# Mem loaded first, biases loaded as rows, two w_mem slices in buffers of their own

## The chip, the cores and the metric

The kernel runs on one core of one Trainium2 chip. The metric is the device time of one execution in microseconds (us). Three runs of the kernel before took 675.11, 677.58 and 680.07 us, so the median is 677.58 us. A difference of about 1% (6.8 us) is what such runs can tell from no change.

## The reference, cut to what matters

The program computes one layer of a hybrid encoder on x (1024 x 1024, float32) and a memory mem (256 x 1024).

```
h    = layer_norm(x, ln_in_g, ln_in_b)
proj = h @ w_in + b_in                 # D_IN = 3912 columns, split among four head groups
       A: gated mixing   B: band attention   C: indexer, top 256 keys, attention   M: attention into mem
km, vm = split(mem @ w_mem_kv, 2)      # w_mem_kv is 1024 x 512
mixed  = concat(ya*silu(a_g), yb*silu(bg), yc*silu(cg), ym*silu(mg))
out    = layer_norm(2**0.25 * h + mixed @ w_out + b_out, ln_g, ln_b)
```

Only the first lines matter here: the norm of x, the product of mem with w_mem_kv, and the first columns of the projection (the indexer's key and head weights, `I_K`, and the first half of the gate of group M, `M_G`). ln_in_b and b_in are added per column of h and of proj. As h and proj are held turned round (columns on the 128 partitions), each bias is a number per partition.

## The kernel before, in words

Every large product is made with three matmuls per 128 rows of contraction: each float32 operand is split into a rounded part and a rest, and high x high, high x low and low x high are accumulated. `wblock` (L194) loads one slice of 128 weight columns (512 KB) into `raw`, a tag with two buffers, and splits it in two halves of 128x512 into `wblk`: ScalarE (ACT) copies the rounded part, GpSimd (POOL) subtracts it (L208). A third slice can be loaded only when POOL has finished with the first.

The work at the start is this. The loop over `FIRST_LOADS` (L359) issues the first transfers on SyncE's queue (SP): row blocks of x (`xt`, 128 rows, 512 KB each), the vector ln_in_g spread over all partitions (`g_in`), two halves of mem (`mt`) and the first two slices of w_mem, in the order x g m x m w x w x. Then come `b_col` (ln_in_b, L368) and `load_biases` (L146): four transfers whose source is read with neighbouring numbers going to neighbouring partitions, so that every number is a piece of 4 bytes; VectorE (DVE) makes `hbias`, half of `bias`, in three instructions.

`mem_parts` turns mem with TensorE (PE) and splits it into mT (ACT copies, DVE subtracts). `x_rows` (L290) norms one row block: two statistics instructions, an aggregate, a scaled subtraction (all DVE), the reciprocal root on POOL (`rs`, two instructions), and a scaling on ACT. `kv_of_mem` multiplies mem with the slices of w_mem; each call with i = 0 loads slices 2 and 3 from inside its loop. `x_parts` (L304) turns four normed row blocks, eight times four transposes into a PSUM bank, and from each bank ACT writes `hTh` and DVE writes `hTl`, with b_col as bias. A half of 512 positions needs all four of its row blocks before the first of its eight columns can be written. `ik_half` and `gate_half` are the first projections; they are called for half 0, then `x_rows` of blocks 4 to 7, the second `x_parts`, and the same projections for half 1.

Loads of x blocks 4 to 7 are kept behind the load of w_mem slice 3 (`issue_after(loads[3])`, L406); their `x_rows` are kept behind the last `hTl` of half 0 (`issue_after(first_half[0])`, L409). The order on each engine is otherwise written by a planner that runs before compilation: it walks the program with its own estimates of durations and takes the instruction with the best priority that is ready, where earlier program text has the better priority and a boost can be given (`high_priority`). Each engine then works through its list in that order and waits where an input is late.

Of the kernel before, what the change touches and what calls it, by code (L numbers as in the profile page):

```python
# [11 lines left out]
F32 = mybir.dt.float32  # L12
# [7 lines left out]
ALU = mybir.AluOpType  # L20
# [4 lines left out]
P = 128  # L25
NB = 8
KT = 8
# [18 lines left out]
OB, LB = 400, 0  # L46
LG_AT = 0
PRELOAD = (6,)
FIRST_LOADS = "xgmxmwxwx"
ML_V = (6,)  # L50
HR_V = 6
LB_V = (7, 6)
# [21 lines left out]
def f32(ap):  # L74
    return ap.bitcast(F32)
# [3 lines left out]
def tile_trunk(ctx, tc, x, mem, ln_in_g, ln_in_b, w_in, b_in, a_ln_g, a_ln_b, a_ws, a_bs,  # L79
               b_rel_rev, t5_table, w_mem, w_out, b_out, ln_g, ln_b, bucket1h, out):  # L80
    nc = tc.nc
    G, SP = nc.gpsimd, nc.sync
# [20 lines left out]
    PE, V, S = Engine(nc.tensor), Engine(nc.vector), Engine(nc.scalar)  # L103

    def run(steps):

        while True:
            try:
                next(steps)
            except StopIteration as e:  # L110
                return e.value

    cp = ctx.enter_context(tc.tile_pool(name="cp", bufs=1))
    gp = ctx.enter_context(tc.tile_pool(name="gp", bufs=1))
# [4 lines left out]
    ident = cp.tile([P, P], F32, name="ident")  # L119
# [8 lines left out]
    def bcast(t, vec):  # L128
        n = vec.shape[-1]
        SP.dma_start(out=t, in_=bass.AP(tensor=vec.tensor, offset=vec.offset, ap=[[0, P], [1, n]]))  # L130
# [5 lines left out]


    col = {}
    bias = cp.tile([P, 31], F32, name="bias")
    hbias = cp.tile([P, 31], F32, name="hbias")  # L140
    spans = ((0, 26, P), (I_K, 1, 72), (M_Q, 4, P))
    for c0, n, _ in spans:
# [1 line left out]
            col[c0 + t * P] = len(col)  # L144

    def load_biases():  # L146
        V.memset(hbias, 0.0)
        for c0, n, m in spans:
            a = col[c0]
            SP.dma_start(out=bias[:m, a:a + n], in_=b_in[c0:c0 + n * m].rearrange("(t p) -> p t", p=m))  # L150
            V.tensor_scalar(hbias[:m, a:a + n], bias[:m, a:a + n], 0.5, None, ALU.mult)

    h_dram = [dp.tile([P, DM], F32, name=f"h_dram{r}") for r in range(NB)]

# [15 lines left out]
    def s4(name, dt=F32R, shape=(P, SEQ)):  # L170
        return gp.tile(list(shape), dt, tag="s4", bufs=S4, name=name)
# [11 lines left out]
    E = ep.enter_context(tc.tile_pool(name="ep", bufs=1))  # L183

    def ev(name, bufs=EV):
        return E.tile([P, 512], F32, tag="ev", bufs=bufs, name=name)

    def bank(tag, name=None):
        return ps.tile([P, 512], F32, tag=tag, bufs=BANKS[tag], name=name or tag)


    loads = []

    def wblock(w, c0, m=P):  # L194

        raw = E.tile([P, KT, P], F32, tag="raw", bufs=2, name="raw")
        loads.append(SP.dma_start(out=raw[:, :, :m], in_=w[:, c0:c0 + m].rearrange("(k p) c -> p k c", p=P)).ins)
        ts = []
        if m < P:
            narrow = [gp.tile([P, 2, KT // 2, m], F32R, tag=tag, bufs=1, name="wnar") for tag in ("planes", "score6")]  # L200
        for q in range(2):
            t = E.tile([P, 2, 4, P], F32R, tag="w", bufs=WB, name="wblk") if m == P else narrow[q]
            r = raw[:, 4 * q:4 * q + 4, :m]
            if WH[0] <= len(loads) < WH[1]:
                G.tensor_scalar(t[:, 0], r, 1.0, 0.0, ALU.mult, ALU.add)
            else:
                S.activation(t[:, 0], r, AF.Copy)
            G.tensor_sub(t[:, 1], r, f32(t[:, 0]))  # L208
            ts.append(t)
        return ts  # L210

    def project(t, a, b, m=P, hi=hh, lo=hl, tag="pp"):

        acc = bank(tag, "acc")
        for k in range(KT):
            wh, wl = t[k // 4][:, 0, k % 4, :m], t[k // 4][:, 1, k % 4, :m]
            PE.matmul(acc[:m, :b - a], wh, hi(k, a, b), start=(k == 0), stop=False)
            PE.matmul(acc[:m, :b - a], wh, lo(k, a, b), start=False, stop=False)
            PE.matmul(acc[:m, :b - a], wl, hi(k, a, b), start=False, stop=(k == KT - 1))
            yield  # L220
        return acc
# [56 lines left out]


    g_in = s4("g_in", F32)  # L280
    b_col = cp.tile([P, KT], F32, name="b_col")
    mT = [s4(f"mT{i}", F32R, (P, 4, 256)) for i in range(4)]

    def x_load(rb):
        tag = ("S", "S", "S", "S", "s4", "score7", "v3", "v3")[rb]
        xt = gp.tile([P, DM], F32, tag=tag, bufs={"S": SB, "v3": 2, "s4": S4}.get(tag, 1), name="xt")
        SP.dma_start(out=xt, in_=x[rb * P:(rb + 1) * P, :])
        return xt

    def x_rows(rb, xt):  # L290

        st = E.tile([P, 2, 6], F32, tag="st", bufs=2, name="st")
        V.bn_stats(st[:, 0], xt[:, :512])
        V.bn_stats(st[:, 1], xt[:, 512:])
        mv = E.tile([P, 2], F32, tag="mv", bufs=2, name="mv")
        V.bn_aggr(mv, st)
        rs = E.tile([P, 1], F32, tag="rs", bufs=2, name="rs")
        with tc.high_priority(offset=BOOST):
            rstd_of(mv[:, 1:2], rs)
        V.scalar_tensor_tensor(xt, xt, mv[:, 0:1], g_in, ALU.subtract, ALU.mult)  # L300
        with tc.high_priority(offset=BOOST):
            S.activation(xt, xt, AF.Copy, scale=rs)

    def x_parts(half, xts):  # L304

        high, rest = hT[half]
        for k in range(KT):
            pt = bank(("pt", "qk")[k % 2], "xT")
            for j in range(4):
                PE.transpose(pt[:, j * P:(j + 1) * P], xts[j][:, k * P:(k + 1) * P], ident)  # L310
            begin = S.activation(high[:, k, :], pt, AF.Identity, bias=b_col[:, k:k + 1])
            end = V.scalar_tensor_tensor(rest[:, k, :], pt, b_col[:, k:k + 1], f32(high[:, k, :]), ALU.add, ALU.subtract)
        return end.ins, begin.ins
# [6 lines left out]
    def mem_parts(r, mt):  # L320
        for q in range(2):
            pt = bank("pt")
            for j in range(4):
                k = 4 * q + j
                PE.transpose(pt[:, j * P:(j + 1) * P], mt[:, k * P:(k + 1) * P], ident)
            src, dst = pt.rearrange("p (a b) -> p a b", a=4), slice(r * P, (r + 1) * P)
            S.activation(mT[q][:, :, dst], src, AF.Copy)
            V.tensor_sub(mT[2 + q][:, :, dst], src, f32(mT[q][:, :, dst]))
# [29 lines left out]
    xts, mts, w_kv = [], [], []  # L358
    for what in FIRST_LOADS:  # L359
        if what == "x":  # L360
            xts.append(x_load(len(xts)))
        if what == "m":
            mts.append(mem_load(len(mts)))
        if what == "w":
            w_kv.append(wblock(w_mem, len(w_kv) * P))
        if what == "g":
            bcast(g_in, ln_in_g)
    SP.dma_start(out=b_col, in_=ln_in_b.rearrange("(t p) -> p t", p=P))  # L368
    load_biases()
    for r in range(2):  # L370
        mem_parts(r, mts[r])
    for rb in range(4):
        x_rows(rb, xts[rb])
    def kv_of_mem(i):

        t = ev("kv")
        for pair in range(2):
            acc = run(project(w_kv[2 * i + pair], 0, 256, P, mhi, mlo))
            S.activation(t[:, pair * 256:pair * 256 + 256], acc[:, :256], AF.Copy)
            if not i:  # L380
                w_kv.append(wblock(w_mem, 256 + pair * P))
        return t

    km = kv_of_mem(0)
    first_half = x_parts(0, xts)
    vm = kv_of_mem(1)


    wik = wblock(w_in, I_K, 72)
    wmg = wblock(w_in, M_G)  # L390
    ikh = s4("ikh")
# [3 lines left out]
    def ik_half(a, b):  # L395
        acc = run(project(wik, a, b, 72))
        bk = col[I_K]
        with tc.high_priority(offset=BOOST):
            for lo in (0, 64):
                S.activation(ikh[lo:lo + 64, a:b], acc[0:64, :], AF.Identity, bias=bias[0:64, bk:bk + 1])  # L400
            S.activation(iwT[64:72, a:b], acc[64:72, :], AF.Identity, bias=bias[64:72, bk:bk + 1])
            for lo in (0, 64):
                V.scalar_tensor_tensor(ikl[lo:lo + 64, a:b], acc[0:64, :], bias[0:64, bk:bk + 1],
                                       f32(ikh[0:64, a:b]), ALU.add, ALU.subtract)

    with tc.issue_after(loads[3]):  # L406
        xts += [x_load(rb) for rb in range(4, NB)]
    ik_half(0, 512)
    with tc.issue_after(first_half[0]):  # L409
        for rb in range(4, NB):  # L410
# [378 lines left out]
    for g in range(4):  # L789
        SP.dma_start(out=bsT[64 * (g % 2):64 * (g % 2) + 64, g // 2, :],  # L790
                     in_=bass.AP(tensor=a_bs.tensor, offset=a_bs.offset + g * P, ap=[[0, 64], [1, P]]))
# [182 lines left out]
    for i, rb in enumerate(RBS):  # L974
        n = (rb + 1) * P
# [85 lines left out]
    for i, rb in enumerate(RBS):  # L1061
        n = (rb + 1) * P
# [241 lines left out]
    for k in range(KT):  # L1304
        hi, lo = [t[:, k % 4, :] for t in wo[k // 4]]
        raw = E.tile([P, DM], F32, tag="raw", bufs=2, name="rawo")
        SP.dma_start(out=raw, in_=w_out[k * P:(k + 1) * P, :])
        for half in range(2):
            c = slice(half * 512, half * 512 + 512)
# [73 lines left out]
```

## Time and profile before

| | |
|---|---|
| median of three runs | 677.58 us |
| the profiled execution | 678.19 us |
| its span in the trace | 676.4 us |
| PE busy | 638.7 us, 94% of the span |
| DVE, ACT, POOL busy | 480.1, 426.4, 354.4 us |
| mean DMA rate over the span | 111 GB/s |

The span is the time between the first and the last instruction in the trace; 1.79 us of the profiled execution lie outside it. PE is TensorE's matmul, SP issues the transfers. A row of the timeline is a run of like instructions on one engine: its start, how long it was busy, the tile written and the tiles read, their shape and count, and in square brackets how long the engine had been idle before and what ended that. A row of the windows gives the busy time and the number of instructions of each engine in a stretch, the clock granted to TensorE (1.00 is 2.4 GHz, 0.50 is 1.2 GHz), the mean busy share of the 16 DMA engines, and the rate.

### The profile page before, as it was taken

The numbers are of one execution on the slowest core, as the hardware profiler recorded it, in microseconds if no ns is written. First come the engines' busy times: TensorE is split into PE (matmuls) and PEld (weight loads), VectorE is DVE, ScalarE is ACT, GpSimd is POOL, SyncE is SP. The second block draws the span as 40 slices with busy tenths as digits, with TensorE's granted clock in tenths as the row PEclk, the third lists the DMA queues.
The fourth block names the chain that finished last, engine by engine and source line by source line (L and its number), as shares of the span: only waits on it lengthen the run. The fifth ranks groups of instructions, "written<-read, shape, count | busy, mean of one in ns | idle before, by whom it ended". The sixth has DMA issues, their size and how long they took to land.

```text
span 676.4 us, 11066 instructions
## 1 busy us (share of the span) xinstructions
PE 638.7 (94%) x3698; PEld 484.5 (72%) x3698; DVE 480.1 (71%) x1165; ACT 426.4 (63%) x947; POOL 354.4 (52%) x354
## 2 busy tenths in 40 slices
PE   4889999899999999989998999999999999999995
PEld 3867776677787677767665776667677777778785
DVE  6584256567867789899889778995567559787535
ACT  4665255547599998776879986466456575356210
POOL 3682321104535886484448535994214776557851
PEclk9999999899999999999999999999999999999999
DMA  9783521012234543554347625645101574225111
GB/s 280 236 296 112 163 57 32 0 48 63 78 110 94 110 117 97 115 123 135 71 101 139 148 74 110 120 82 150 31 16 44 180 230 145 72 88 193 66 62 63
DMA packets 121669, 75.30 MB, mean 111 GB/s; under 512 B 58976, under 2 KB 111500, under 8 KB 121612
## 3 DMA queue, kind: packets, MB, share of 16 engines
q1 hardware_dynamic: 121612, 74.59, 40.5%
q8 instruction: 29, 0.48, 0.3%
q14 instruction: 28, 0.23, 0.1%
HBM read 46.44 MB, written 17.64 MB: 95 GB/s over the span
## 4 chain that ended last, share of the span: by engine, by line
PE 50%; DVE 13%; POOL 11%; ACT 11%; issue 8%; DMA 6%; SPq 0%; POOLq 0%; DVEq 0%; ACTq 0%
PE acc L94 36%; PE qk L94 6%; ACT jka L94 4%; PE pv L94 4%; POOL wblk L208 3%; DMA pT<-sc 3%; PE pt L94 2%; DVE jk L94 2%; POOL sc L545 2%; ACT sc L94 1%; DMA raw<-in_w_in 1%; POOL sc L546 1%; DVE sc L94 1%; DMA xt<-in_x 1%; DMA hr<-h_dram 1%
## 5 line engine op out<-in xcount | busy, mean ns | idle before, releaser
L94 PE MATMUL acc<-hTh,wblk 128*128 128x512 f32 (+1 forms) x960 | 317.4, 400 | 6.4 <-DVE iql L94 2.6
L94 PEld LDWEIGHTS acc<-hTh,wblk 128*128 128x128 f32 x960 | 177.2, 189 | 52.5 <-issue 6.1
L94 PE MATMUL acc<-hTl,wblk 128*128 128x512 f32 (+1 forms) x480 | 190.4, 397 | 0.0
L208 POOL TENSOR_TENSOR wblk<-raw,wblk 128x512 fp32r<-128x512 f32 x72 | 99.7, 1388 | 123.2 <-ACT wblk L94 120.0
L94 ACT ACTIVATE jka<-score,cand 128x768 int8<-128x768 f32 (+2 forms) x93 | 96.5, 1038 | 16.2 <-DVE cand L94 15.4
L94 PEld LDWEIGHTS acc<-hTl,wblk 128*128 128x128 f32 x480 | 90.9, 189 | 20.6 <-issue 4.0
L94 PEld LDWEIGHTS <-pT 128*128 128x128 f16 x656 | 45.7, 98 | 31.7 <-issue 17.9
L94 DVE SCALAR_TENSOR_TENSOR score<-relu,iw,score 128x384 f32<-128x384 f32 (+5 forms) x42 | 43.7, 1058 | 23.9 <-ACT relu L94 22.1
L94 PE MATMUL pv<-v,pT 128*128 128x192 bf16 (+1 forms) x528 | 54.3, 234 | 4.8 <-DMA pT<-sc 4.0
L94 ACT ACTIVATE wblk<-raw 128x512 fp32r<-128x512 f32 x72 | 44.5, 627 | 22.6 <-PE acc L94 12.8
L546 POOL TENSOR_TENSOR sc<-sc 128x512 f16<-128x512 f32 (+4 forms) x48 | 56.0, 1172 | 2.3
L94 PE MATMUL acc<-woh,mh 128*128 128x512 f32 (+1 forms) x144 | 55.3, 384 | 0.0
L94 PE MATMUL acc<-wol,mh 128*128 128x512 f32 (+1 forms) x144 | 53.5, 372 | 0.0
L94 PE MATMUL acc<-woh,ml 128*128 128x512 f32 (+1 forms) x144 | 53.5, 373 | 0.0
L94 ACT ACTIVATE relu<-qk 128x384 f32<-128x384 f32 (+2 forms) x80 | 35.9, 530 | 24.1 <-PE qk L94 23.8
L545 POOL TENSOR_SCALAR sc<-sc 128x512 f16<-128x512 f32 (+4 forms) x48 | 33.4, 698 | 30.6 <-ACT sc L94 28.6
L94 ACT ACTIVATE sc<-sc,nb 128x640 f32<-128x640 f32 (+7 forms) x64 | 46.5, 729 | 1.2
L94 ACT ACTIVATE pT<-pt 128x512 f16<-128x512 f32 (+3 forms) x48 | 22.5, 485 | 31.0 <-PE pt L94 30.7
L94 ACT ACTIVATE o<-o,ri 128x64 f32<-128x64 f32 x96 | 28.1, 341 | 17.8 <-DVE o L94 17.6
L94 DVE TENSOR_SCALAR_CACHE_REDUCE jk<-planes,lo 128x384 bf16<-128x384 uint16 (+2 forms) x48 | 35.6, 742 | 1.1
L94 DVE TENSOR_SCALAR_CACHE_REDUCE jk<-planes,cand 128x384 bf16<-128x384 bf16 (+2 forms) x45 | 33.5, 744 | 1.1
L94 DVE TENSOR_REDUCE o<-pv 128x128 f32<-128x384 f32 x48 | 26.4, 549 | 9.7 <-PE pv L94 9.6
(204 smaller groups left out, 1238.4 us busy)
## 6 DMA issues: line engine op xcount, KB each, us to landing
raw<-in_w_in SPq DMA_DIRECT2D x32, 512.0 KB, 3.8
xt<-in_x SPq DMA_DIRECT2D x8, 512.0 KB, 4.7
h_dram<-xt SPq DMA_DIRECT2D x8, 512.0 KB, 5.6
gate<-t SPq DMA_DIRECT2D x16, 256.0 KB, 2.1
rawo<-in_w_out SPq DMA_DIRECT2D x8, 512.0 KB, 3.7
hr<-h_dram SPq DMA_DIRECT2D x8, 512.0 KB, 5.2
out<-hr SPq DMA_DIRECT2D x7, 512.0 KB, 2.6
gate<-gate SPq DMA_DIRECT2D x48, 64.0 KB, 2.1
```

The lines of the kernel that those rows point to most:

```text
L94: ins = op(*a, **k)
L208: G.tensor_sub(t[:, 1], r, f32(t[:, 0]))
L545: G.tensor_scalar(high, sc[:, :n], 1.0, 0.0, ALU.mult, ALU.add)
L546: G.tensor_sub(rest, sc[:, :n], high)
```

## The change

The first transfers go out as m m w x g x w x x. The four bias transfers become four with contiguous rows of 512 bytes into a tile of 39 rows (8 rows of ln_in_b, 31 of b_in); PE turns this tile, DVE copies the result to `cols`, which holds `b_col` and `bias`, and makes `hbias` with one instruction. w_mem slices 2 and 3 are loaded before `kv_of_mem` is called, each as two transfers of 256 KB into tiles that are used later in the program for other things (`jk`, `vt`, `near`), so they wait for no `raw` buffer. The rests of w_mem slices 0 and 1 are subtracted by DVE (`len(loads) < 3`), all others by POOL as before. The loads of x blocks 4 to 7 are written right behind these loads, without `issue_after(loads[3])`. Nothing else is changed.

```diff
-FIRST_LOADS = "xgmxmwxwx"
+FIRST_LOADS = "mmwxgxwxx"
...
-    bias = cp.tile([P, 31], F32, name="bias")
+    cols = cp.tile([P, KT + 31], F32, name="cols")
+    b_col, bias = cols[:, :KT], cols[:, KT:]
...
     def load_biases():
-        V.memset(hbias, 0.0)
+        rows = ev("rows")[:KT + 31, :P]
+        V.memset(rows, 0.0)
+        SP.dma_start(out=rows[:KT], in_=ln_in_b.rearrange("(t p) -> t p", p=P))
         for c0, n, m in spans:
-            a = col[c0]
-            SP.dma_start(out=bias[:m, a:a + n], in_=b_in[c0:c0 + n * m].rearrange("(t p) -> p t", p=m))
-            V.tensor_scalar(hbias[:m, a:a + n], bias[:m, a:a + n], 0.5, None, ALU.mult)
+            a = KT + col[c0]
+            SP.dma_start(out=rows[a:a + n, :m], in_=b_in[c0:c0 + n * m].rearrange("(t p) -> t p", p=m))
+        return rows
+
+    def turn_biases(rows):
+        pt = bank("pv", "bT")
+        n = KT + 31
+        PE.transpose(pt[:, :n], rows, ident[:n, :n])
+        V.tensor_copy(cols, pt[:, :n])
+        V.tensor_scalar(hbias, bias, 0.5, None, ALU.mult)
...
-    def wblock(w, c0, m=P):
+    def wblock(w, c0, m=P, places=None):
...
+        if places:
+            raws = [gp.tile([P, 4, P], F32, tag=tag, bufs=bufs, name="raw") for tag, bufs in places]
+            for q in range(2):
+                loads.append(SP.dma_start(out=raws[q], in_=src[:, 4 * q:4 * q + 4]).ins)
...
-            G.tensor_sub(t[:, 1], r, f32(t[:, 0]))
+            (V if len(loads) < 3 else G).tensor_sub(t[:, 1], r, f32(t[:, 0]))
...
-    SP.dma_start(out=b_col, in_=ln_in_b.rearrange("(t p) -> p t", p=P))
-    load_biases()
+    rows = load_biases()
     for r in range(2):
         mem_parts(r, mts[r])
+    turn_biases(rows)
...
-            if not i:
-                w_kv.append(wblock(w_mem, 256 + pair * P))
         return t
 
+    for pair in range(2):
+        w_kv.append(wblock(w_mem, 256 + pair * P, places=((("jk", 1), ("vt", 1)), (("near", 2), ("near", 2)))[pair]))
+    xts += [x_load(rb) for rb in range(4, NB)]
     km = kv_of_mem(0)
...
-    with tc.issue_after(loads[3]):
-        xts += [x_load(rb) for rb in range(4, NB)]
```

## Rows read from the trace of the kernel before

**Rows 1.** The page's first part: busy time and share of the span.
```profile
PE 638.7 (94%) x3698; PEld 484.5 (72%) x3698; DVE 480.1 (71%) x1165; ACT 426.4 (63%) x947; POOL 354.4 (52%) x354
```
**Rows 2.** Windows of 25 us: the three at the start, one later.
```profile
0.00:25.00 25.00, 15.00 (x93) 13.94 (x94) 14.50 (x46) 12.03 (x18) 14.29 (x20) 0.93 0.84 239
25.00:50.00 25.00, 21.04 (x126) 16.42 (x124) 19.52 (x27) 17.54 (x29) 15.98 (x16) 1.00 0.88 298
50.00:75.00 25.00, 23.37 (x121) 18.01 (x122) 11.37 (x21) 12.99 (x24) 6.76 (x6) 1.00 0.41 136
75.00:100.00 25.00, 25.00 (x158) 19.27 (x158) 9.08 (x12) 10.78 (x25) 6.44 (x5) 1.00 0.36 101
```
**Rows 3.** Timeline of PE, 0 to 75 us.
```profile
15.05 2.68 PE L94 MATMUL acc<-mT,wblk 128*128 128x256 f32 x11 [0.87 <-POOL wblk L208]
25.55 1.66 PE L94 MATMUL acc<-mT,wblk 128*128 128x256 f32 x12
33.67 0.46 PE L94 MATMUL acc<-hTh,wnar 128*72 128x512 f32 x1 [2.04 <-ACT wnar L94]
50.97 0.50 PE L94 MATMUL acc<-hTh,wblk 128*128 128x512 f32 x1 [1.26 <-ACT hTh L94]
```
**Rows 4.** Timeline of SP's queue, 0 to 75 us.
```profile
10.44 0.43 SPq L368 DMA_DIRECT2D b_col<-in_ln_in_b  x1
10.91 5.78 SPq L150 DMA_DIRECT2D bias<-in_b_in  x3
17.35 4.43 SPq L197 DMA_DIRECT2D raw<-in_w_mem_kv  x2
21.84 2.06 SPq L287 DMA_DIRECT2D xt<-in_x  x4
24.79 10.88 SPq L197 DMA_DIRECT2D raw<-in_w_in  x3
```
**Rows 5.** Windows of 3 us.
```profile
12.00:15.00 3.00, 1.12 (x6) 0.46 (x3) 3.00 (x5) 2.93 (x6) 2.92 (x4) 1.00 1.10 370
15.00:18.00 3.00, 2.95 (x14) 2.96 (x15) 2.96 (x5) 0.98 (x2) 3.00 (x3) 0.52 0.95 16
```
**Rows 6.** Timeline of DVE, 0 to 75 us.
```profile
9.11 1.29 DVE L94 BATCH_NORM_STATS2 st<-xt 128x6 f32<-128x512 f32 x2 [1.32 <-DMA xt<-in_x]
10.31 1.27 DVE L94 TENSOR_TENSOR mT<-pt,mT 128x512 fp32r<-128x512 f32 x2
15.56 1.76 DVE L94 SCALAR_TENSOR_TENSOR xt<-xt,mv,g_in 128x1024 f32<-128x1024 f32 x1
18.95 1.28 DVE L94 SCALAR_TENSOR_TENSOR xt<-xt,mv,g_in 128x1024 f32<-128x1024 f32 x1
33.22 2.46 DVE L94 BATCH_NORM_STATS2 st<-xt 128x6 f32<-128x512 f32 x4
41.45 4.27 DVE L94 SCALAR_TENSOR_TENSOR xt<-xt,mv,g_in 128x1024 f32<-128x1024 f32 x2
45.65 1.49 DVE L94 SCALAR_TENSOR_TENSOR ikl<-acc,bias,ikh 64x512 fp32r<-64x512 f32 x2
49.85 0.69 DVE L94 SCALAR_TENSOR_TENSOR t<-t,xh 128x512 f32<-128x512 f32 x1 [2.71 <-ACT t L94]
58.96 0.68 DVE L94 TENSOR_TENSOR km<-kv,km 128x512 fp32r<-128x512 f32 x1
```
**Rows 7.** Timeline of ACT, 0 to 75 us.
```profile
25.38 1.16 ACT L94 ACTIVATE wblk<-raw 128x512 fp32r<-128x512 f32 x2 [1.45 <-DMA raw<-in_w_mem_kv]
26.44 2.98 ACT L94 ACTIVATE hTh<-xT,b_col 128x512 fp32r<-128x512 f32 x5
50.24 2.99 ACT L94 ACTIVATE hTh<-xT,b_col 128x512 fp32r<-128x512 f32 x5
```
**Rows 8.** Timeline of POOL, 0 to 75 us.
```profile
5.71 0.23 POOL L134 TENSOR_SCALAR rs<-mv 128x1 f32<-128x1 f32 x1 [4.42 <-DVE mv L94]
16.21 1.20 POOL L134 TENSOR_SCALAR rs<-mv 128x1 f32<-128x1 f32 x1
```

More of the change, by code (lines that the diff above doesn't have):

```diff
@@ L192, in tile_trunk @@
     loads = []
-    def wblock(w, c0, m=P):
-        raw = E.tile([P, KT, P], F32, tag="raw", bufs=2, name="raw")
-        loads.append(SP.dma_start(out=raw[:, :, :m], in_=w[:, c0:c0 + m].rearrange("(k p) c -> p k c", p=P)).ins)
+    def wblock(w, c0, m=P, places=None):
+        src = w[:, c0:c0 + m].rearrange("(k p) c -> p k c", p=P)
+        if places:
+            raws = [gp.tile([P, 4, P], F32, tag=tag, bufs=bufs, name="raw") for tag, bufs in places]
+            for q in range(2):
+                loads.append(SP.dma_start(out=raws[q], in_=src[:, 4 * q:4 * q + 4]).ins)
+        else:
+            raw = E.tile([P, KT, P], F32, tag="raw", bufs=2, name="raw")
+            loads.append(SP.dma_start(out=raw[:, :, :m], in_=src).ins)
+            raws = [raw[:, 4 * q:4 * q + 4, :m] for q in range(2)]
         ts = []
@@ L202, in wblock @@
             t = E.tile([P, 2, 4, P], F32R, tag="w", bufs=WB, name="wblk") if m == P else narrow[q]
-            r = raw[:, 4 * q:4 * q + 4, :m]
+            r = raws[q]
             if WH[0] <= len(loads) < WH[1]:
@@ L280, in tile_trunk @@
     g_in = s4("g_in", F32)
-    b_col = cp.tile([P, KT], F32, name="b_col")
     mT = [s4(f"mT{i}", F32R, (P, 4, 256)) for i in range(4)]
```

## The prediction

> **What bounds the kernel now.** I read the page's busy shares first: PE is busy 94% of the span, the next engine 71% [rows 1]. So time can only come from the stretches in which PE waits. The windows of 25 us say where a change at the start can reach: PE works 15.0 of the first 25 us, 21.0 of the second, 23.4 of the third and all of the fourth [rows 2]. That is 15.6 us without a matmul in 75, and the reader is to see that the first two windows hold 14 of them. From about 51 us on PE runs with hardly a gap, so what moves that point moves the end, unless a later order changes.
>
> Then the timelines, each for what sets the start. PE's shows three waits: for POOL's split of the first weights, for the first slice of w_in (2.04 us, up to 33.67), and for the second half's `hTh` (up to 50.97) [rows 3]. SP's shows why w_in was late: the three element-wise bias transfers hold the queue 5.78 us, to 16.69; the two slices of w_mem then wait for `raw` buffers, to 21.78; x blocks 4 to 7 follow, and w_in goes out only from 24.79 [rows 4]. The 3 us windows show the same in the DMA engines: 370 GB/s before the bias pieces, 16 GB/s at a busy share of 0.95 while they move [rows 5]. DVE's timeline shows a second chain. It works without a gap from 9.11 to 20.23, the end of block 3's subtraction; it is at half 0's `hTl` until 33.22; then it norms blocks 4 to 7, from 33.22 to 45.72 [rows 6]. ACT's first `hTh` of a half comes at 26.44 and 50.24, so 6.2 and 4.5 us behind the end of DVE's norms, and at 26.44 it stands behind a split that waited 1.45 us for w_mem slice 3 [rows 7].
>
> **The change part by part.** *Bias rows.* Gone from SP: 0.43 + 5.78 us of issue and some 3 us of DMA time [rows 4, 5]. Added: four issues, each like `b_col`'s 0.43 [rows 4], so 1.7 us, a PE transpose and two small DVE instructions. No row shows a transfer of 512-byte rows this small; its issue lies between 0.43 and the 1.9 us that an element-wise one of b_in took on the mean (5.78 / 3); I take 0.43, since `b_col` with its 1024 pieces already needed no more. The result is first needed by `hTh`, near 26 us, so some 8 us of cover hide it. The new waits are PE's transpose on the rows and DVE's copy on PE: were the rows late, w_mem's matmuls would stand behind the first and the norms of blocks 0 to 3 behind the second, and the lateness would be paid in full. The DVE part, two small instructions, takes the place of `hbias` (below).
>
> *Halves.* Slices 2 and 3 now come as two transfers of 256 KB each. With several transfers in the queue the 512 KB ones moved at 370 GB/s [rows 5], and the halves stand in the same full queue; I price them at nothing, at most two more issues of 0.43 us. The Trainium skill, "DMA: Bandwidth & Descriptors", section Bandwidth, says that smaller transfers get a smaller part of the peak because of a fixed cost each; by that, slices 2 and 3 would land later by about 2 us each, an estimate from its figure of 2 us per DMA, which none of these rows shows while others are in flight.
>
> *Own buffers, loads first.* Nine transfers of 0.524 MB stand ahead of the biases in both kernels; they filled the DMA engines to 15 us. With no hole behind them, six more (slices 2 and 3, x blocks 4 to 7) and the w_in slices need 3.4 MB at 370 GB/s [rows 5], so w_in's first slice lands near 25 us, not 33. SP now issues x blocks 4 to 7 (2.06 us [rows 4]) ahead of w_in as before, so that order costs nothing new. x blocks 4 to 7 themselves gain nothing by landing early: their norms stay behind the last `hTl`, and at 33.22 they did not wait for data [rows 6]. The gain is that `ik_half` can run while `hTh` is written.
>
> *DVE.* This is the chain that I sum. In the new order x block 0 is fourth, and the fourth transfer landed near 9.1 us (DVE's wait for the fourth one, x block 1, ended at 9.11 [rows 6]). Before, block 0 had been normed by then; now four blocks are to come. The stretch from 9.11 to 20.23 held three blocks and four `mT` subtractions (twice 1.27 [rows 6]), so a block is (11.1 - 2.5) / 3 = 2.86 us, small instructions such as `hbias` included; four are 11.4. The two `mT` subtractions of the second half of mem add 1.3. Four weight subtractions come from POOL; DVE has none to show, but `km` has the same shape, from SBUF, at 0.68 [rows 6], or 0.63 in a row of several as `mT`; I take 2.5, with bounds of 2.5 and, stretched as 1.76 against 1.28 [rows 6], 3.7. Block 3 ends at 9.1 + 11.4 + 1.3 + 2.5 = 24.3, **4.1 us later** than 20.23.
>
> *The lag behind it.* ACT no longer stands behind a late slice 3. What must follow is block 3's `rs`, its scaling (1024 columns, as many as the two splits that took 1.16 [rows 7]) and one transpose: 2.0 us instead of 6.2, bounds 1.5 and 6.2. First `hTh` at 26.3, 0.1 earlier. Before, w_mem's last matmuls sat between the transposes and stretched eight columns to 6.8 us (26.44 to 33.22 [rows 6, 7]); w_mem's product is over by then now, so I take 6.2, about 0.75 a column as the `t` row with the same shape [rows 6]: half 0 is done at 32.5, **0.7 us earlier**.
>
> *Second half.* Blocks 4 to 7 took 12.5 us; in them two subtractions took 4.27 where 2.56 was to be expected [rows 6], beside POOL's splits. Those splits come earlier now, so I take off 1.0 of the 1.7: 11.5. But `ikl` (1.49) and the gate's `t` (0.69), behind the norms before [rows 6], are ready earlier and go between: 13.7. So the norms end at 46.2, 0.5 later than 45.72. The lag to the next `hTh` was 4.5 us, in which ACT also did the gate and a split [rows 7]; those are done, so 2.0: `hTh` of half 1 at 48.2, **2.0 us earlier** than 50.24. In the gap that PE now has between 38 and 48 the planner may put the first piece of an indexer query, 24 matmuls of 256 columns, 3.3 us at the 1.66 us for 12 [rows 3]; I count half, 1.6. **Sum: -3.6 us**, between -7 (rival A) and +5 (both lags as before, rival C). PE's added transpose and POOL's four subtractions less lie on no path of this sum. The profiled execution was 678.19, 0.6 above the median; the sum is taken from the median: 677.6 - 3.6 = **674.0**.
>
> **The rivals.** *A, PE keeps all of it (0.28).* `ik_half` may start with the first `hTh`, 26.5 instead of 33.67, 7.2 us [rows 3]. If DVE's norms of blocks 4 to 7 come in time, by little contention and `ikl` behind them, all 7.2 stay: 670.4. For: PE is the bound; against: DVE's 12.5 us of norms stay serial behind `hTl`.
>
> *B, POOL and DVE collide earlier (0.17).* Before, POOL split slices 2 and 3 while DVE was idle or at `hTl`; they now land near 17 and 18 us, in the middle of the norms of blocks 2 and 3. There a subtraction takes up to 4.27 / 2 = 2.1 instead of 1.28, twice 0.9, and POOL's `rs` 1.20 instead of 0.23 [rows 6, 8], twice 1.0; 3.8 us later in all, which eats the gain: 677.6 - 3.6 + 3.8 = 677.8. The Trainium skill, "SBUF — State Buffer", section SBUF: two separate sides, has the rule for it: DVE with two SBUF inputs and GpSimd lock each other out for a whole instruction. The trace agrees in these rows.
>
> *C, slower: the lags stay (0.15).* DVE's block 3 ends 4.1 us later. If ACT's list, written by the planner from estimated landings, again puts other work in front of the scalings, the lags stay 6.2 and 4.5: first `hTh` at 30.5, half 0 done at 36.7, norms at 50.4, second `hTh` at 54.9, 4.7 us later, and PE's gap is no longer there to fill: 677.6 + 4.7 = 682.3. The two lags are 4.0 in my sum and 10.7 before; with the 3.6 gained at 4.0, it is slower from 7.6 on. For: ACT stood so at 25.38 [rows 7]; against: slice 3 is there some 7 us earlier.
>
> *That the loads do not come earlier* would need SP to wait on something in front of w_in; the first tenants of `jk`, `vt`, `near` have nobody to wait for, so I give it no chance of its own.
>
> **How the numbers follow.** My forecast has 0.40. About 1% (6.8 us) can be told from no change, so faster means under 670.8, slower over 684.4. Under 670.8 lie most of A (0.20 of its 0.28) and the tail of the forecast, 0.06, since the planner writes a new order for the whole program and a few us either way are open: 0.26. Over 684.4 lie the tail of C (0.09, the same re-planning on top of it) and 0.03 of B and the forecast: 0.12. Within 1%: 0.62. The range goes from 667.5, which leaves a quarter of A outside, to 681.5, which leaves half of C and a little of the rest outside: 0.18 in all.
>
> **What the new profile would show.** Bias issues under 2 us on SP and no stretch of 16 GB/s at 15 to 18 us; w_in's first slice there near 25; block 3's subtraction ending near 24.3 on DVE; first `hTh` at 26.3 and 48.2; PE without a wait for `wnar`; from 75 us on the same rows 3 to 4 us earlier. I am wrong if block 3 ends near 20 (then A), if DVE's subtractions near 20 us take 2 us (B), if the first `hTh` comes after 29 us (C), or if the start gains and PE's later windows lose it.

## The result and the profile after

The changed kernel takes **684.39 us** (median of six runs, 682.22 to 685.80) against 677.49 us for six runs of the kernel before beside it: ratio 1.0079, 95% interval 1.0049 to 1.0108. It is slower by 0.8%, where the forecast was 674.0 us, range 667.5 to 681.5. The profiled execution took 684.31 us, its span is 682.5 us, 6.1 more than before. Two executions far from the rest of their runs, of 3440 and 774 us, are left out of the ratios below.

The page's first part, after (answers to [rows 1]):

```profile
PE 643.9 (94%) x3699; PEld 487.7 (71%) x3699; DVE 483.4 (71%) x1168; ACT 426.8 (63%) x947; POOL 349.6 (51%) x350
```

Take PE's busy time from the span in both kernels: it was idle 37.7 us before and 38.6 after. Of the 6.1 us, only 0.9 are idle time; 5.2 are busy time, for one instruction more. The windows show where (answers to [rows 2]; the columns are the same):

```profile
0.00:25.00 25.00, 16.37 (x108) 14.45 (x109) 17.07 (x49) 11.41 (x19) 10.07 (x17) 1.00 0.98 330
25.00:50.00 25.00, 19.81 (x101) 14.61 (x99) 17.40 (x26) 16.25 (x28) 13.33 (x16) 0.91 0.63 213
50.00:75.00 25.00, 22.18 (x106) 17.71 (x107) 12.11 (x19) 13.16 (x22) 6.72 (x6) 0.82 0.21 71
...
46.00:48.00 2.00, 0.08 (x1) 0.09 (x2) 1.26 (x2) 1.94 (x3) 0.00 (x0) 1.00 0.60 211
...
56.00:58.00 2.00, 2.00 (x10) 1.90 (x9) 2.00 (x4) 1.66 (x3) 0.00 (x0) 0.50 0.43 121
```

The first window gained: 15 more matmuls, 330 GB/s instead of 239. The second and third lost 25 and 15, and their mean granted clock is 0.91 and 0.82, where it was 1.00. PE's idle time there is 2.4 us longer, of which the first window gives back 1.4; but by 75 us PE has 24 matmuls fewer behind it (313, 337 before). PE nearly stands from 45.7 to 54.1 us; in the course of it, at 48.8, the clock falls from 2.4 to 1.2 GHz, and it is still there when the work is back, up to 59.0. Timeline of PE, after (answers to [rows 3]):

```profile
31.52 0.54 PE L94 MATMUL acc<-hTh,wnar 128*72 128x512 f32 x1 [0.54 <-ACT wnar L94]
...
58.04 0.63 PE L94 MATMUL acc<-hTh,wblk 128*128 128x256 f32 x2
59.20 0.40 PE L94 MATMUL acc<-hTh,wblk 128*128 128x256 f32 x2
```

PE waits 0.54 us for `wnar` instead of 2.04. The other two rows show what the clock costs: a pair of the same matmuls takes 0.63 us at 58.04 and 0.40 at 59.20, when it has come back.

The start went as the change meant it. The timeline of SP, after (answers to [rows 4]):

```profile
8.27 0.74 SPq L151 DMA_DIRECT2D rows<-in_ln_in_b  x1
9.06 1.65 SPq L154 DMA_DIRECT2D rows<-in_b_in  x3
...
18.36 0.38 SPq L215 DMA_DIRECT2D raw<-in_w_in  x1
```

The biases hold SP for 2.4 us instead of 6.2, and the first slice of w_in is issued 6.4 us earlier. DVE, POOL and ACT show what became of that. Timeline of DVE, after (answers to [rows 6]):

```profile
19.41 2.05 DVE L94 SCALAR_TENSOR_TENSOR xt<-xt,mv,g_in 128x1024 f32<-128x1024 f32 x1
21.47 1.27 DVE L94 SCALAR_TENSOR_TENSOR xt<-xt,mv,g_in 128x1024 f32<-128x1024 f32 x1
...
37.73 0.39 DVE L94 BATCH_NORM_AGGREGATE mv<-st 128x2 f32<-128x12 f32 x2
46.72 1.50 DVE L94 SCALAR_TENSOR_TENSOR ikl<-acc,cols,ikh 64x512 fp32r<-64x512 f32 x2 [2.66 <-ACT iwT L94]
48.38 2.43 DVE L94 SCALAR_TENSOR_TENSOR xt<-xt,mv,g_in 128x1024 f32<-128x1024 f32 x2
```

Timeline of POOL, after (answers to [rows 8]):

```profile
20.35 2.46 POOL L134 TENSOR_SCALAR rs<-mv 128x1 f32<-128x1 f32 x2
22.78 1.26 POOL L227 TENSOR_TENSOR wblk<-raw,wblk 128x512 fp32r<-128x512 f32 x1
24.00 1.08 POOL L135 TENSOR_TENSOR rs<-rs,mhalf 128x1 f32<-128x1 f32 x2
...
38.25 3.42 POOL L227 TENSOR_TENSOR wblk<-raw,wblk 128x512 fp32r<-128x512 f32 x2 [2.66 <-ACT wblk L94]
41.64 1.37 POOL L134 TENSOR_SCALAR rs<-mv 128x1 f32<-128x1 f32 x2
42.98 1.08 POOL L135 TENSOR_TENSOR rs<-rs,mhalf 128x1 f32<-128x1 f32 x2
...
49.66 2.28 POOL L227 TENSOR_TENSOR wblk<-raw,wblk 128x512 fp32r<-128x512 f32 x1
51.91 1.01 POOL L135 TENSOR_TENSOR rs<-rs,mhalf 128x1 f32<-128x1 f32 x1
```

Timeline of ACT, after (answers to [rows 7]):

```profile
24.59 1.15 ACT L94 ACTIVATE xt<-xt,rs 128x1024 f32<-128x1024 f32 x1 [3.71 <-POOL rs L135]
28.15 2.99 ACT L94 ACTIVATE hTh<-xT,cols 128x512 fp32r<-128x512 f32 x5
37.55 1.15 ACT L94 ACTIVATE wblk<-raw 128x512 fp32r<-128x512 f32 x2 [2.97 <-DMA raw<-in_w_in]
43.57 1.15 ACT L94 ACTIVATE xt<-xt,rs 128x1024 f32<-128x1024 f32 x1 [4.87 <-POOL rs L135]
44.63 1.36 ACT L94 ACTIVATE ikh<-acc,cols 64x512 fp32r<-64x512 f32 x2
52.95 1.15 ACT L94 ACTIVATE xt<-xt,rs 128x1024 f32<-128x1024 f32 x1 [1.69 <-POOL rs L135]
54.66 3.00 ACT L94 ACTIVATE hTh<-xT,cols 128x512 fp32r<-128x512 f32 x5
```

Follow the second half through the three. (`ikh` and `iwT` are what ACT writes of the first projection, `ik_half`; `ikl` is DVE's rest of it. A root is POOL's two instructions, L134 and then L135.) DVE has the aggregates of blocks 4 and 5 at 38.1. Their roots are done only at 44.1: in POOL's list the two splits of the first query slice stand ahead of them, and those wait for ACT, which waits for that slice's load. The kernel before waits for the same load, but there the two roots come first. Timeline of POOL, kernel before:

```profile
35.26 3.54 POOL L208 TENSOR_TENSOR wblk<-raw,wblk 128x512 fp32r<-128x512 f32 x2
38.77 1.33 POOL L134 TENSOR_SCALAR rs<-mv 128x1 f32<-128x1 f32 x2
40.07 1.07 POOL L135 TENSOR_TENSOR rs<-rs,mhalf 128x1 f32<-128x1 f32 x2
41.11 3.53 POOL L208 TENSOR_TENSOR wblk<-raw,wblk 128x512 fp32r<-128x512 f32 x2
```

In the kernel after, ACT stands 4.87 us on that root with its scaling of block 4; behind the scaling in its list stand `ikh` and `iwT`; DVE's `ikl` waits for them until 46.72; behind `ikl` stand the subtractions of blocks 6 and 7, done at 50.81 instead of 45.72. Then one more split, 2.28 us, stands on POOL ahead of the last instruction of block 7's root, and the second half's `hTh` begins at 54.66 instead of 50.24.

### The profile page after: what moved, and what is told of

It is laid out like the page before. It is cut to its first block, busy times and chain, and to the rows that moved or that the text cites. A ratio compares the mean times of both kernels' runs of the same rounds, so it can differ in the third digit from the quotient of the medians.

```text
span 682.5 us, 11075 instructions
## 1 busy us (share of the span) xinstructions
PE 643.9 (94%) x3699; PEld 487.7 (71%) x3699; DVE 483.4 (71%) x1168; ACT 426.8 (63%) x947; POOL 349.6 (51%) x350
## 4 chain that ended last, share of the span: by engine, by line
PE 54%; DVE 13%; ACT 10%; POOL 8%; issue 7%; DMA 7%; SPq 0%; POOLq 0%; DVEq 0%; ACTq 0%
PE acc L94 38%; PE qk L94 7%; PE pv L94 5%; ACT jka L94 4%; DMA pT<-sc 4%; PE pt L94 2%; DVE jk L94 2%; POOL wblk L227 2%; ACT sc L94 1%; POOL sc L563 1%; DMA xt<-in_x 1%; DVE bit L94 1%; DVE sc L94 1%; ACT wblk L94 1%; DVE score L94 1%
## 5 line engine op out<-in xcount | busy, mean ns | idle before, releaser
L227 POOL TENSOR_TENSOR wblk<-raw,wblk 128x512 fp32r<-128x512 f32 x68 | 94.2, 1389 | 126.9 <-ACT wblk L94 125.4
L94 ACT ACTIVATE jka<-score,cand 128x768 int8<-128x768 f32 (+2 forms) x93 | 96.6, 1038 | 16.2 <-DVE cand L94 15.4
L94 PEld LDWEIGHTS <-pT 128*128 128x128 f16 x656 | 46.4, 99 | 31.7 <-issue 19.2
L94 ACT ACTIVATE wblk<-raw 128x512 fp32r<-128x512 f32 x72 | 44.7, 629 | 18.5 <-PE acc L94 10.8
L94 ACT ACTIVATE o<-o,ri 128x64 f32<-128x64 f32 x96 | 28.1, 341 | 17.7 <-DVE o L94 17.4
```

Source lines behind the costliest of these rows:

```text
L94: ins = op(*a, **k)
L227: (V if len(loads) < 3 else G).tensor_sub(t[:, 1], r, f32(t[:, 0]))
```

## The experiments

The planner writes the engine lists anew for every edit and may change any of them, so each run is read by its landmarks in its own trace (us; "half 0" is the end of the last `hTl` of half 0, "`hTh` 1" the first `hTh` of half 1, "between" the time from the one to the other, "query" the first `iql`, DVE's rest of the first indexer query; the span is that of the one profiled execution; ratio to the kernel before on the same chip). "Between" is the landmark to compare, since half 0 itself ends at different times in runs whose lists are the same up to there:

| run | half 0 | `hTh` 1 | between | query | span | ratio, 95% |
|---|---|---|---|---|---|---|
| before | 33.30 | 50.24 | 16.94 | 68.60 | 676.4 | |
| after | 35.43 | 54.66 | 19.23 | 74.35 | 682.5 | 1.0079 (1.0049 to 1.0108) |
| after_root_on_dve | 34.78 | 49.88 | 15.10 | 67.92 | 675.7 | 0.9996 (0.9980 to 1.0011) |
| before_root_on_dve | 33.00 | 50.23 | 17.23 | 71.13 | 684.6 | 1.0096 (1.0074 to 1.0117) |
| after_splits_behind_roots | 35.18 | 49.25 | 14.07 | 67.75 | 674.7 | **0.9974** (0.9957 to 0.9991) |
| after_slice3_behind_root3 | 35.26 | 54.62 | 19.36 | 74.70 | 685.3 | 1.0048 (1.0023 to 1.0073) |
| after_queries_behind_root7 | 36.74 | 50.80 | 14.06 | 69.21 | 676.1 | 0.9970 (0.9945 to 0.9996) |
| before_mem_first_only | 34.98 | 50.17 | 15.19 | 69.12 | 680.8 | 1.0003 (0.9980 to 1.0026) |
| before_bias_rows_only | 34.56 | 50.62 | 16.06 | 68.99 | 676.2 | 0.9972 (0.9950 to 0.9994) |
| after_ikh_ahead_of_scaling | 35.22 | 50.58 | 15.36 | 68.96 | 675.2 | 1.0009 (0.9986 to 1.0032) |
| after_ikl_behind_block7 | 37.14 | 54.30 | 17.16 | 74.24 | 685.2 | 1.0107 (1.0072 to 1.0143) |
| after_both_pins_and_ikl | 36.17 | 50.37 | 14.20 | 68.58 | 678.2 | 1.0034 (1.0014 to 1.0055) |
| after_splits_on_pool | 35.64 | 53.00 | 17.36 | 72.11 | 681.7 | 1.0037 (1.0014 to 1.0059) |
| after_gap_filled | 35.18 | 55.23 | 20.05 | 75.28 | 684.2 | 1.0133 (1.0084 to 1.0182) |

**The root off POOL.** First: does the late root on POOL make the loss? In the two kernels the root is replaced by a linear stand-in on DVE (not the root; it leaves POOL's two instructions out).

```diff
-            rstd_of(mv[:, 1:2], rs)
+            V.tensor_scalar(rs, mv[:, 1:2], -0.5, 1.5, ALU.mult, ALU.add)
```

> The changed kernel, but in the norms of x the two POOL instructions of the reciprocal root are left out; DVE writes a linear stand-in (1.5 - 0.5 variance) with one 128x1 instruction. Theory (the root on POOL is the lost time: it stands behind weight splits and waits for DVE's subtractions, and ACT and DVE queue up behind it): first hTh falls from 28.15 to about 25.5 us, half 1's from 54.66 to about 48, the clock row of 0.50 from 49 to 59 us is gone, and the time falls by 5 to 8 us below the changed kernel, to 677 to 679 us (ratio to the kernel before 0.993 to 1.003). Rival (the planner's new order after 75 us loses it): under 2 us gained, ratio 1.005 to 1.010. Rival (mem first: x starts 5 us later, DVE is the bound): hTh stays behind 27 us.

The whole loss is gone, as expected, and so is the stretch at half clock from 49 to 59 us. `hTh` 1 is 4.8 us earlier, where about 6.7 were expected, and half 0's first `hTh` came at 27.48, not 25.5.

> The kernel before with the same stand-in for the root. Theory: here the root waits less (first hTh stood behind a late slice of w_mem, and 1.0 us at 46.49), so it gains 1 to 3 us, ratio 0.995 to 1.000, less than the changed kernel gains. If it gains as much as the changed kernel does, the root is a cost of both and does not explain the difference.

The control missed: slower by 1%. Its `hTh` 1 comes when it did before, and the loss lies behind it. Windows of that run:

```profile
50.00:55.00 5.00, 5.00 (x22) 4.49 (x22) 3.77 (x6) 3.53 (x7) 1.35 (x2) 0.50 0.52 194
65.00:70.00 5.00, 3.68 (x17) 2.68 (x15) 1.03 (x2) 3.73 (x6) 1.29 (x1) 1.00 0.38 102
70.00:75.00 5.00, 3.82 (x12) 2.53 (x13) 2.77 (x6) 1.10 (x3) 1.45 (x1) 0.80 0.29 99
```

PE is at half clock throughout 50 to 55 and idle again for 2.5 us between 65 and 75, around the first query: another list, another hole. That is read from one trace; no run isolates it. A shorter root is thus no gain by itself.

**POOL's order alone.** The root stays; POOL's subtractions are only kept behind roots, slice 3 of w_mem behind block 3's, the first two query slices behind block 7's.

```diff
-    loads = []
+    loads, roots, behind = [], [], {6: 3, 9: 7, 10: 7}
...
+            if len(loads) in behind:
+                tc.add_manual_dep(ins, roots[behind[len(loads)]].name, mybir.DependencyInfo(
...
```

The key is the number of the load (6 ends w_mem slice 3, 9 and 10 are the first two query slices), the value the block whose root goes first.

> The changed kernel, complete, with POOL's order pinned: the splits of w_mem slice 3 stand behind block 3's root, those of the first two indexer query slices behind block 7's root. Theory: POOL's order is the larger part of the lost time; first hTh at 26 to 27 us (two roots still wait for DVE's subtractions), half 1's at 49 to 51, 3 to 6 us below the changed kernel, ratio 1.000 to 1.004. If the wait of the roots for DVE alone is the cause, under 1.5 us gained. Rival (later order): no gain.

It beats both kernels: 676.55 us, 0.26% under the kernel before and 1.0% under the changed one (0.9974 / 1.0079, each against the kernel before), so more than the 1.000 to 1.004 that was expected; `hTh` 1 came where expected, the first `hTh`, 27.69, later. Timeline of POOL, then of ACT, in this run:

```profile
37.83 1.45 POOL L134 TENSOR_SCALAR rs<-mv 128x1 f32<-128x1 f32 x2 [1.90 <-DVE mv L94]
39.24 1.08 POOL L135 TENSOR_TENSOR rs<-rs,mhalf 128x1 f32<-128x1 f32 x2
47.47 3.82 POOL L227 TENSOR_TENSOR wblk<-raw,wblk 128x512 fp32r<-128x512 f32 x3
```

```profile
39.83 1.15 ACT L94 ACTIVATE xt<-xt,rs 128x1024 f32<-128x1024 f32 x1 [1.11 <-POOL rs L135]
40.89 1.36 ACT L94 ACTIVATE ikh<-acc,cols 64x512 fp32r<-64x512 f32 x2
49.25 3.00 ACT L94 ACTIVATE hTh<-xT,cols 128x512 fp32r<-128x512 f32 x5
```

The roots run as soon as DVE has the aggregates, the scaling and `ikh` come 3.7 us earlier than after, `hTh` 1 5.4. The next two runs take the two pins one by one.

```diff
-    loads, roots, behind = [], [], {6: 3, 9: 7, 10: 7}
+    loads, roots, behind = [], [], {6: 3}
```

```diff
-    loads, roots, behind = [], [], {6: 3, 9: 7, 10: 7}
+    loads, roots, behind = [], [], {9: 7, 10: 7}
```

> The changed kernel with only the first half's order pinned on POOL: the splits of w_mem slice 3 behind block 3's root. Theory (what costs is the second half: the splits of the first two indexer query slices stand ahead of the roots of blocks 4, 5 and 7): little gained, hTh of half 1 stays at 53 to 55 us, ratio to the kernel before 1.005 to 1.009. Rival (the roots of blocks 2 and 3 in the first half are the cause): ratio 0.996 to 1.001.

> The changed kernel with only the second half's order pinned on POOL: the splits of the first two indexer query slices behind block 7's root. Theory: the whole gain of the two pins together, hTh of half 1 at 49 to 50 us, ratio 0.996 to 1.000. Rival (first half): ratio 1.004 to 1.009.

All of the gain is in the second pin, though that run's half 0 was done 1.3 us later than after's. With the first alone, `hTh` 1 stays at 54.62.

The run with the second pin alone is the cleanest comparison of all. Its lists of DVE and ACT are those of the changed kernel from the first instruction to the last, PE's differs only where a few neighbours change places, the first at 360 us, and on POOL nothing has moved but the splits of the two query slices; on SP one load of w_in goes out five transfers later. Timeline of POOL in this run:

```profile
40.80 1.08 POOL L135 TENSOR_TENSOR rs<-rs,mhalf 128x1 f32<-128x1 f32 x2
...
49.02 4.16 POOL L227 TENSOR_TENSOR wblk<-raw,wblk 128x512 fp32r<-128x512 f32 x3
```

With no more moved than that, "between" falls from 19.23 to 14.06 us and the ratio from 1.0079 to 0.9970.

**One part of the change at a time.** First the order of the loads alone, on the kernel before.

```diff
-FIRST_LOADS = "xgmxmwxwx"
+FIRST_LOADS = "mmwxgxwxx"
```

> The kernel before with only the new order of the first loads. Its POOL list has four weight splits in front of the roots of blocks 4 and 5, as the changed kernel has, so by the theory it is slower than the kernel before: hTh of half 1 at 53 us or later, ratio 1.004 to 1.012. Rival (only the four parts together do it, by DVE's extra work): ratio 0.998 to 1.002.

No change in time, so a miss that corrected the theory. Its POOL list has the same fault, its ACT list has not. Timeline of POOL, then of ACT, in this run:

```profile
38.84 3.54 POOL L208 TENSOR_TENSOR wblk<-raw,wblk 128x512 fp32r<-128x512 f32 x2 [1.66 <-ACT wblk L94]
42.35 0.40 POOL L134 TENSOR_SCALAR rs<-mv 128x1 f32<-128x1 f32 x2
```

```profile
39.19 1.36 ACT L94 ACTIVATE ikh<-acc,bias 64x512 fp32r<-64x512 f32 x2
43.30 2.19 ACT L94 ACTIVATE xt<-xt,rs 128x1024 f32<-128x1024 f32 x2 [1.65 <-POOL rs L135]
```

The root is as late as after (done at 43.8), but `ikh` stands ahead of the scaling that waits for it, so DVE's `ikl` and blocks 6 and 7 (done at 46.78) do not wait. A late root costs what stands behind its reader.

Second, the bias rows alone: the new `load_biases`, `turn_biases` and `cols` on the kernel before.

```diff
-    load_biases()
+    rows = load_biases()
...
+    turn_biases(rows)
```

> The kernel before with only the biases as rows. Its POOL list keeps the roots of blocks 4 and 5 in front of the query splits, so the theory expects no loss: hTh of half 1 at 47 to 50 us, ratio 0.993 to 1.001, the SP queue free of the 5.78 us. Rival (bias rows cost by PE's and DVE's new waits): ratio above 1.003.

A gain of 0.28%, in the expected range and just clear of no change; `hTh` 1 came at 50.62, not at 47 to 50. Where the gain comes from is not shown: half 0, `hTh` 1 and the query come no earlier than before. The biases hold SP for 1.24 us here, but then w_mem slices 2 and 3 wait for `raw` as they did (issued from 16.23, before from 17.35), and w_in goes out from 26.54, before from 24.79. So it was not the bias transfers alone that kept w_in late.

**The corrected theory.** The changed kernel with POOL as it is, but ACT's scalings of blocks 4 to 7 kept behind `ikh` and `iwT`.

```diff
-            S.activation(xt, xt, AF.Copy, scale=rs)
+            if rb < 4:
+                S.activation(xt, xt, AF.Copy, scale=rs)
+            else:
+                with tc.issue_after(S.ik):
+                    S.activation(xt, xt, AF.Copy, scale=rs)
...
     ik_half(0, 512)
+    S.ik = S.last
```

> The changed kernel with POOL's list unchanged in front of the roots of blocks 4 and 5, but with ikh and iwT of half 0 in front of block 4's scaling in ACT's list. Theory now (the late root costs because ikh stands behind the scaling that waits for it, DVE's ikl behind ikh, and the subtractions of blocks 6 and 7 behind ikl): ikl at 43 to 44 instead of 46.7, block 7's subtraction done at 47 to 48 instead of 50.8, hTh of half 1 near 51, ratio to the kernel before 1.000 to 1.004. Rival (the late roots cost by themselves): hTh of half 1 stays at 53 to 55, ratio 1.005 to 1.009.

It hit: `ikh` at 41.24, `ikl` at 43.78, block 7's subtraction done at 47.81, `hTh` 1 at 50.58, no loss. In its list block 7's root also stands ahead of the late split, so this run has both last links mended.

Then only DVE's `ikl` of half 0 kept behind block 7's subtraction, with ACT and POOL as they are.

```diff
-    ik_half(0, 512)
+    ik_rest = ik_half(0, 512)
...
+    with tc.issue_after(V.last):
+        ik_rest()
```

> The changed kernel with only DVE's ikl of half 0 moved behind block 7's subtraction, as it stands in the kernel before. Theory: DVE no longer waits 2.7 us in front of blocks 6 and 7; their subtractions end at 46 to 47, but block 7's root may still stand behind a split; hTh of half 1 at 49 to 51, ratio 0.998 to 1.003. Rival (late roots by themselves): ratio 1.005 to 1.009.

A miss. DVE's last subtraction ends 2.5 us earlier, at 48.33, but `hTh` 1 only 0.4. Half 0 was done 1.7 us later in this execution; "between" is 17.16, so 2.1 us of the 5.2 are gained, and the time of the run is lost again behind that: the first query comes as late as after, the second at 83.19 (79.43 after). Timeline of ACT in this run:

```profile
45.28 1.15 ACT L94 ACTIVATE xt<-xt,rs 128x1024 f32<-128x1024 f32 x1 [4.91 <-POOL rs L135]
...
52.58 1.15 ACT L94 ACTIVATE xt<-xt,rs 128x1024 f32<-128x1024 f32 x1
```

ACT's first scaling waits as long as after, and its list behind it then has no slack: block 7's is at 52.58, with no wait of its own. So DVE's wait is one branch, ACT's backlog the other; the late root feeds both. Pins and `ikl` together:

```diff
-    loads = []
+    loads, roots, behind = [], [], {6: 3, 9: 7, 10: 7}
...
+    with tc.issue_after(V.last):
+        ik_rest()
```

> The changed kernel with the splits behind the roots (as in after_splits_behind_roots) and ikl behind block 7's subtraction. Theory: both waits gone, hTh of half 1 at 47.5 to 49, ratio 0.993 to 0.998. If the pins alone already removed the wait, the same as after_splits_behind_roots, 0.997.

A miss: `hTh` 1 comes at 50.37, not at 47.5 to 49, "between" is that of the pins alone (14.20 and 14.07), and the second query comes at 75.97 (72.82 with the pins alone), since PE is busy only 2.98 us of the five behind 65. With the pins there is nothing left for `ikl` to gain, and the new list has a new hole.

**The change's other suspect.** DVE's weight subtractions given back to POOL.

```diff
-            (V if len(loads) < 3 else G).tensor_sub(t[:, 1], r, f32(t[:, 0]))
+            G.tensor_sub(t[:, 1], r, f32(t[:, 0]))
```

> The changed kernel with the splits of w_mem slices 0 and 1 back on POOL. Its POOL list still has four splits in front of the roots of blocks 4 and 5. Theory: not faster than the changed kernel, ratio 1.004 to 1.012. Rival (the four subtractions added to DVE are the cost): DVE's block 3 ends 2 us earlier and the ratio falls to 0.998 to 1.003.

Block 3's subtraction ends 2.3 us earlier, at 20.40; its first `hTh` comes at 28.07, as after. DVE's added work does not set half 0. But the loss is about half of the changed kernel's (1.0037, just under the expected range), and `hTh` 1 comes 1.7 us earlier. Timeline of ACT in this run:

```profile
50.12 2.31 ACT L94 ACTIVATE xt<-xt,rs 128x1024 f32<-128x1024 f32 x2
```

Blocks 4 and 5 wait for their late roots as after (4.99 us on ACT), `ikl` starts at 46.76 and the last subtraction ends at 50.84, also as after; but the late split no longer stands ahead of block 7's root, and the scaling of block 7 follows that of block 6 without a wait. So this run puts the price of that one split at about 1.9 us of "between" (17.36 for 19.23). Whether the four subtractions on DVE cost something besides is not shown.

**Clock or wait.** PE's gaps from 45 to 54 us filled with repeated transposes, to hold the clock up while the lists of the other engines stay.

```diff
-                PE.transpose(pt[:, j * P:(j + 1) * P], xts[j][:, k * P:(k + 1) * P], ident)
+                for _ in range((4, 4, 3, 1)[j] if half and k < 5 else 1):
+                    PE.transpose(pt[:, j * P:(j + 1) * P], xts[j][:, k * P:(k + 1) * P], ident)
```

> The kernel after with 40 transposes more: the first five columns of blocks 4 and 5 are turned four times instead of once, those of block 6 three times (same result, same tiles). They stand on PE just where it waits for the scalings of blocks 5, 6 and 7; the lists of POOL, ACT and DVE are those of the kernel after up to the second half's first hTh, two neighbours on ACT apart. Theory 'clock': by 75 us PE has 24 instructions fewer behind it than before, but only 1.05 us more idle time, so most of the loss is the stretch at half clock from 49 to 59 us, which the gaps bring on. With the gaps filled the clock stays up, the first hTh stays near 54.7, and the ratio falls by 2 to 4 us from 1.0079 to 1.002-1.005. Theory 'wait': the scalings that come late are the whole loss, the clock is beside it: the ratio stays at 1.006-1.010. If the added transposes themselves get in the way (they do not fit the gaps), hTh comes after 55.5 and the ratio goes over 1.010.

Inconclusive: the ratio is over 1.010, as for transposes that get in the way, but `hTh` 1 comes at 55.23, under the 55.5 that went with it. Windows of this run:

```profile
50.00:52.00 2.00, 1.83 (x17) 1.56 (x15) 2.00 (x2) 0.74 (x1) 2.00 (x2) 1.00 0.28 102
52.00:54.00 2.00, 0.32 (x3) 0.10 (x2) 0.67 (x2) 1.30 (x2) 0.67 (x1) 1.00 0.77 303
56.00:58.00 2.00, 2.00 (x8) 1.81 (x9) 2.00 (x4) 2.00 (x4) 0.07 (x1) 0.50 0.26 76
```

The clock held to 55, but one gap stayed (52 to 54) and the restart at 56 was at half clock again; later PE waited 2.2 us of the five behind 70 in a new list. What the clock costs by itself stays open. The run with the second pin alone, which does the same work as the changed kernel in lists that differ hardly anywhere but on POOL, gives a division: of the 6.4 us of span between the two, 3.6 are PE's idle time (38.6 and 35.0) and 2.8 its busy time (643.9 and 641.1).

## Why the prediction was wrong, step by step

**The step that failed is "the lag behind it".** I let the first `hTh` follow DVE's last subtraction of a half by 2.0 us, since ACT would no longer stand behind a late slice. Measured: 28.15 - 22.74 = 5.4 and 54.66 - 50.81 = 3.85. I read ACT's list for what stood in front of the scalings and not POOL's for what stood in front of the roots, though the root was in my own list of "what must follow". In POOL's new list a 1.26 us split stands ahead of the last instruction of block 3's root and a 2.28 us split ahead of that of block 7's. For the second half it is shown that POOL's order is the cause: with pins on POOL alone that lag is 2.2 us (47.08 to 49.25), and the loss is gone. Half 0's lag stays at 4.25 with them (23.44 to 27.69), so POOL's list is only a part of it. The rest has to do with a sentence of the same step, "w_mem's product is over by then now": it was not. Timeline of PE, after:

```profile
26.38 1.45 PE L94 MATMUL acc<-mT,wblk 128*128 128x256 f32 x10
27.67 0.71 PE L94 MATMUL xT<-ident,xt 128*128 128x128 f32 x5
```

Block 3's scaling ends at 27.06 on ACT, and its transposes begin at 27.67, behind ten matmuls of w_mem. With the pins ACT stands 1.15 us ahead of the first `hTh` for the same reason. No run isolates this part.

**"Second half", the 13.7 us of norms, failed with it.** They took 15.4 (35.43 to 50.81). I had let `ikl` go between at its own 1.49; it came with a wait of 2.66 for ACT, which stood behind POOL's root. What each link is worth can be read from "between" in runs whose half 0 ended within 0.5 us: 19.2 in the changed kernel; 17.4 where only the late split is gone from block 7's root (after_splits_on_pool); 15.4 where in addition `ikh` stands ahead of the scaling (after_ikh_ahead_of_scaling); 14.1 where the roots come first (after_splits_behind_roots).

**Rival C** had the outcome (slower, lags stay) and its bound: the lags sum to 9.25, over the 7.6 from which it decides. It had the wrong queue: ACT waited on POOL, not behind splits of its own; and its sign, a first `hTh` after 29 us, did not show (28.15). **Rival B's** collision and its sign are in the rows: `rs` twice 1.2 us beside two subtractions, of which the first took 2.05. The Trainium skill, "SBUF — State Buffer", section SBUF: two separate sides, says that DVE with two SBUF inputs and a GpSimd instruction that reads SBUF lock each other out for a whole instruction; the rows agree even for a 128x1 operation. It is a part of half 0's lag only.

**The other steps.** *Bias rows:* 2.4 us of issue, not 1.7, all covered: the copy to `cols` took 0.14 us at 19.21, 9 us before its use. The price was near enough. That these transfers were what kept w_in late was not: alone, without them, w_in goes out no earlier (before_bias_rows_only). *Halves:* priced at nothing; the DMA engines moved 408 and 308 GB/s at 12 to 15 and 15 to 18 us, where they had 370 and 16 [rows 5]. The Trainium skill's smaller share of the peak for smaller transfers ("DMA: Bandwidth & Descriptors", section Bandwidth) is not visible in these rows, and no run isolates it. *Loads first:* the first w_in slice was issued at 18.36 and landed 8.3 us behind its issue, near 27 for the forecast 25, but its gain was not passed on: ACT splits it only at 30.99, behind five `hTh`, so its `raw` buffer came free at 33.1, and the third slice of w_in, the one that the splits at 38.25 wait for, could be issued only then (ACT's wait for it ended at 37.55, 39.77 before). *DVE:* block 3 ended at 22.74, not 24.3; of the 1.6, 1.3 are a weight and an `mT` subtraction that were done before 9.17. The price of a weight subtraction, 2.5 for four, was right (0.64 to 0.69 each). *Half 0* took 7.3 us from its first `hTh`, not 6.2: two splits (0.81 and 1.18) stand between them on ACT.

**The account:** half 0 was done 2.9 us later than in my sum (35.43 against 32.5); from there to `hTh` 1 it took 19.2 instead of 15.7, 3.5 more. The 1.6 us for PE's filled gap did not come back either, and restarting at half clock cost 1.3 (the 19 matmuls of the query that follow one another from 55.90 took 3.8 us; the same 19 took 2.5 in after_splits_behind_roots). Together 9.3 of the 9.7 between the -3.6 of the sum and the +6.1 of the span.

## What to carry to other kernels

When a planner writes the lists, a change of loads or of one engine's work can move instructions on engines that it does not touch; before summing a lag, ask for each small link of it, a 128x1 root too, what else is ready for that engine at that time, and what stands behind its reader. If the changed order makes a short link wait behind bulk work, pin the bulk work behind the link: that turned a loss of 0.8% into a gain of 0.26%. A landmark that moves by 5 us is a cause only when an edit of that link alone moves it back, since swings of up to 1% came from new holes elsewhere in three of these runs.

## What the runs showed of the hardware

PE's low clock was paid as busy time. In the changed kernel the granted clock was 0.50 in four stretches before the end (31.7 to 35.1, 48.8 to 59.0, 127.3 to 130.7 and 369.7 to 373.1 us), and PE worked 16.5 us in them; in the kernel before in two (15.1 to 18.5, 120.9 to 124.3), and it worked 6.7. If work takes twice as long there, an estimate from the two levels, that is 4.9 us of the 5.2 by which PE's busy time grew. Only the second stretch comes with the pause of PE from 45.7 to 54.1; PE worked 6.3 us in it, so it stands for 3.1 of them at most. With that pause mostly filled by transposes (after_gap_filled) the clock stayed at 1.00 to 55.7.

The first of the root's two instructions on POOL, 128x1, took 1.2 us beside DVE's subtractions (20.35) and 0.23 alone (5.71 in [rows 8]).

The same first loads, in lists that are equal up to there, brought the first `hTh` at 28.15 in the changed kernel and at 29.44 (after_queries_behind_root7) or 29.84 (after_ikl_behind_block7), so that differences of 1 to 2 us in one profile's start are not to be explained by an edit. In the first of these the granted clock was 0.50 from 14.8 to 18.2 us, where it was 1.00 in the changed kernel.
